# The first four k tiles of a transformer stage scaled and shifted one at a time

## The chip, the cores and the metric

The kernel runs on one core of one Trainium2 chip. The metric is device time in microseconds (us) of one execution. A core has five engines that run side by side, each in the order of its own queue: TensorE (PE: matrix products into PSUM, with PEld its weight loads), VectorE (DVE), ScalarE (ACT), GpSimd (POOL) and SyncE (SP), which here only issues DMA transfers. An engine that needs another's result waits at a semaphore, and everything behind that instruction in its queue waits too.

## The reference, cut to what matters

The reference is a two-layer transformer with a latent stream `lat` and a context stream `cx`, each of 256 tokens and 1024 features; layer 0 has a short convolution as its mixer, layer 1 attention. All of it is float32. The change touches only the first feed-forward block of layer 0, whose input is normalised and modulated:

```
def _rms(t, g):
    t32 = t.astype(jnp.float32)
    y = t32 * lax.rsqrt(jnp.mean(t32 * t32, axis=-1, keepdims=True) + NORM_EPS)
    return y.astype(t.dtype) * g

def _modulate(t, g, shift, scale):
    return _rms(t, g) * (1 + scale) + shift

def _swiglu(h, w13, w2):
    gte, up = jnp.split(h @ w13, 2, axis=-1)
    return (jax.nn.silu(gte) * up) @ w2

mod = (jax.nn.silu(c) @ mod_w[i] + mod_b[i]).reshape(bsz, 3, 3, 1, D_MODEL)
lat = lat + 0.5 * mod[:, 0, 2] * _swiglu(_modulate(lat, norm_g[i, 0], mod[:, 0, 0], mod[:, 0, 1]), ...)
```

Shift and scale are themselves a product: a vector (`silu(c)` for `lat`, `silu(c_ctx)` for `cx`) by 1024 columns of `mod_w` each. So before the first product of the feed-forward block can run, the kernel must have the token norms, and of shift and scale the features that this product reads.

## The kernel before, in words

Features lie on the 128 partitions, so 1024 features are eight k tiles (`KT`), and the 512 tokens of both streams lie side by side in a row (`T2`; `s` = 0 for `lat`, 1 for `cx`). Every float32 matrix is split into a rounded high part and the remainder (`split`, or steps H and D below), and a product is three matmuls: high by high, high by low, low by high.

The first stage multiplies three blocks of 256 hidden columns of `ffn_w13` (i = 0, 1, 2; each a gate half `pg` and an up half `pu`) by all eight k tiles: 3 x 8 x 2 x 3 = 144 matmuls of 128x128 weights by 512 columns. Its order on PE, DVE, ACT and SP is written out by hand, in the string `FIRST_STEPS` (L39), and played under a manual schedule (L1135 to L1139). A step is a letter and digits:

- `L ch q` (`mod_load`, L928) issues on SP the load of two tiles of `mod_w`, 512 KB each: for ch = 1 the scale, for ch = 0 the shift, of the two k tiles 2q and 2q + 1. `R i hf` (`first_raw`) issues the load of half a weight block, 512 KB.
- `P ch q` (`mod_pe`, L934) multiplies them on PE: eight matmuls whose weights are only 32 columns wide (`sccol`), each in one of four column strips of the array (`tile_position=(0, g)`), by 256 columns. The profile shows two records for each of them, as float32 goes through in two passes. The four strips leave partial sums on different partitions.
- `T q` (`mod_turn`, L950) copies these sums out of PSUM (ACT, `row`, L954), turns them into columns and adds up the strips with two small matmuls (PE, L956), and adds the bias (DVE, L963): A00 is 1 + scale, B00 the shift, two k tiles at a time.
- `X` (`first_inv`, L1012) takes the sums of squares and makes the reciprocal norms: a square root (ACT, L1015), a reciprocal (DVE, L1019), two small matmuls for each stream that spread it over all partitions (PE, L287), and a copy out of PSUM for each stream (ACT, `ris`, L1023).
- `U q` (`scale_q`, L1028) multiplies x by gain and reciprocal norm (DVE, `hr`, L1033) for two k tiles and both streams. `N q j` (`norm_one`, L1038) applies A00 and B00 to one k tile: the rounded high part `hh` (ACT, L1043), the exact value (DVE L1049 or ACT L1053), the remainder `hl` (DVE, L1057).
- `H i p` rounds a quarter of weight block i (ACT, `wh`, L1108), `D i p` takes its remainder (DVE, `wl`, L1110), `W` does both.
- `h`, `w`, `l` with i, q, j are two of the stage's matmuls each (L1070), for block i and k tile 2q + j: high by high, low weights by `hh`, high weights by `hl`. `M i q` is all twelve of a pair of k tiles. `F n` is n matmuls on constants that only keep PE busy.

Each engine takes its instructions in the order of the string. SP's loads are gated: `first_sums` (L968) writes one column of the first `mod_w` tile from x (L995), so no load of `mod_w` is issued before that part of x has landed. After the stage, a planner orders DVE and ACT; PE goes on with block i = 3 (L136 to L138).

Of the kernel before, what the change touches and what calls it, by code (L numbers as in the profile page):

```python
# [36 lines left out]


FIRST_STEPS = (  # L39
# [5 lines left out]
)  # L45


# [1 line left out]
def hybrid_kernel(ctx: ExitStack, tc: tile.TileContext, a: dict, out: bass.AP):  # L49
    nc = tc.nc  # L50
# [4 lines left out]
    gp = ctx.enter_context(tc.tile_pool(name="gp", bufs=8))  # L55
    tp = ctx.enter_context(tc.tile_pool(name="tp", bufs=2))
# [32 lines left out]
    eps_t = const.tile([P, 1], F32, name="eps_t", tag="eps_t")  # L89
# [194 lines left out]
    def rms_all(pq, ri):  # L284

        for i in range(2):
            every.append(nc.tensor.matmul(  # L287
                pq[:, i * P : i * P + P], ri[:, i : i + 1].to_broadcast([P, P]), ident,
                start=True, stop=True,
            ).ins)  # L290
        return pq[:, :S]
# [23 lines left out]
    def hot(s, dt=F32R):  # L315
        return hop.tile([P, 1024], dt, name=nm(s), tag="hop")
# [11 lines left out]
    class Beside:  # L328
# [12 lines left out]
    def beside(t):  # L341
        return t[:, :S], t[:, S:], t
# [569 lines left out]
    h32 = {}  # L912
# [7 lines left out]
    A00 = const.tile([P, KT, 2], F32, name="A00", tag="A00")  # L920
    B00 = mod_tile(0, 0)
    sb1 = const.tile([P, KT], F32, name="sb1", tag="sb1")
    def both(t):
        return t.unsqueeze(2).to_broadcast([P, 2, 2])

    rows = {}

    def mod_load(ch, q):  # L928
        if (ch, q) not in rows:
            rows[ch, q] = [hot("pm", F32) for _ in range(2)]  # L930
        for i in range(2):
            nc.sync.dma_start(rows[ch, q][i], a["mod0"][ch, q, :, i * 1024 : i * 1024 + 1024])

    def mod_pe(ch, q):  # L934


        raws = rows[ch, q]
        if ch:
            rows[q] = psum("pr") if q == 0 else psmall("pr")
        pr = rows[q]  # L940
        c = 2 if ch else 0
        for k in range(KT):
            g = 32 * (k % 4)
            o = k % 4 * S
            nc.tensor.matmul(
                pr[g : g + 32, :S], sccol[:, k, c : c + 32], raws[k // 4][:, o : o + S],
                start=(ch == 1 and k < 4), stop=(ch == 0 and k >= 4), tile_position=(0, g),
            )

    def mod_turn(q):  # L950

        pr = rows[q]
        row = tp.tile([P, T2], F32, name=nm("row"), tag="gm", bufs=3)
        nc.scalar.copy(row[:, :S], pr[:, :S])  # L954
        for j in range(2):
            nc.tensor.matmul(  # L956
                pr[:, S + 4 * j : S + 4 * j + 4], row[:, j * P : j * P + P], rowsum,
                start=True, stop=True,
            )
        k2 = slice(2 * q, 2 * q + 2)  # L960
        turned = pr[:, S : S + 8].rearrange("p (k c v) -> p k c v", k=2, c=2)
        for ch in (1, 0):
            nc.vector.tensor_tensor(  # L963
                out=(A00 if ch else B00)[:, k2, :], in0=turned[:, :, 1 - ch, :],
                in1=both(sb1[:, k2] if ch else modb[:, 0, k2]), op=ALU.add,
            )

    def first_sums():  # L968

        pq = psmall("ss")  # L970
        sq = []

        def square(k, eng):
            tag = "gm" if k % 4 < 2 else "sg"
            t = tp.tile([P, T2], F32, name=nm("sq"), tag=tag, bufs=3)
            if eng is nc.vector:
                nc.vector.tensor_tensor(out=t, in0=x[:, k, :], in1=x[:, k, :], op=ALU.mult)
            else:
                nc.scalar.activation(out=t, in_=x[:, k, :], func=AF.Square)
            sq.append(t)  # L980

        def add():
            a, b = sq[-2:]
            nc.vector.tensor_tensor(out=a, in0=a, in1=b, op=ALU.add)
            n = len(sq)
            for i in range(4):
                nc.tensor.matmul(
                    pq[:, i * P : i * P + P], a[:, i * P : i * P + P], ones,
                    start=(n, i) == (2, 0), stop=(n, i) == (KT, 3), skip_group_check=True,
                )  # L990

        square(0, nc.scalar)
        square(1, nc.vector)
        rows[1, 0] = [hot("pm", F32) for _ in range(2)]
        nc.vector.tensor_copy(rows[1, 0][0][:, :1], x[:, 2, :1])  # L995
        add()
        square(2, nc.scalar)
        square(3, nc.scalar)
        add()
        nc.scalar.activation(out=sccol[:, :, 2:4], in_=ccol, func=AF.Silu)  # L1000
        square(4, nc.scalar)
        square(5, nc.vector)
        add()
        square(6, nc.scalar)
        square(7, nc.scalar)
        add()
        nc.vector.tensor_scalar(
            out=sb1, in0=modb[:, 0, KT : 2 * KT], scalar1=1.0, scalar2=None, op0=ALU.add
        )
        return pq  # L1010

    def first_inv(pq):  # L1012

        rs = tp.tile([P, 4], F32, name=nm("rs"), tag="rs4", bufs=1)
        nc.scalar.activation(  # L1015
            out=rs, in_=pq[:, ::P], func=AF.Sqrt, scale=1.0 / D, bias=eps_t
        )
        ri = tp.tile([P, 4], F32, name=nm("ri"), tag="ri4", bufs=1)
        nc.vector.reciprocal(ri, rs)  # L1019
        t = tp.tile([P, T2], F32, name=nm("ris"), tag="ris", bufs=1)  # L1020
        for s in range(2):
            ris.append(t[:, s * S : s * S + S])
            nc.scalar.copy(ris[s], rms_all(psmall("ri") if s else pq, ri[:, 2 * s : 2 * s + 2]))  # L1023

    def raw_of(k, s):
        return h32[k // 2, s][:, (k % 2) * S : (k % 2) * S + S]

    def scale_q(q):  # L1028
        for s in range(2):
            h32[q, s] = gp.tile([P, T2], F32, name=nm("hr"), tag="gl" if s else "gh")  # L1030
        for k in range(2 * q, 2 * q + 2):
            for s in range(2):
                nc.vector.scalar_tensor_tensor(  # L1033
                    out=raw_of(k, s), in0=x[:, k, s * S : s * S + S],
                    scalar=normg[:, 0, 0, k : k + 1], in1=ris[s], op0=ALU.mult, op1=ALU.mult,
                )
# [22 lines left out]
            )  # L1059

    pps = {}
    ris = []

    def first_part(lo):
        def part(i, q, j):
# [16 lines left out]
    ws, gs0, raws, cut = {}, [], {}, {}  # L1082
# [18 lines left out]
    def first_w(part):  # L1101
# [21 lines left out]
        "W": first_w("W"),  # L1123
        "H": first_w("H"),
        "D": first_w("D"),
        "X": lambda: first_inv(pqs),
        "U": scale_q,
        "N": norm_one,
        "h": first_part(0),
# [134 lines left out]
    pqs = pss.tile([P, T2], F32, tag="sm", name="pqs")  # L1264
# [107 lines left out]
    pq = [q_proj(0)]  # L1372
# [17 lines left out]
    for kv in range(KVH):  # L1390
# [7 lines left out]
        out=scq, in0=rq[:, :16], scalar1=float(P) ** -0.5, scalar2=None, op0=ALU.mult  # L1398
# [131 lines left out]
def _layout(inp):  # L1530
    f = lambda k: np.asarray(inp[k])
    d = {}

    def kp(w, width):
# [8 lines left out]
    ccol = d["c2"].reshape(2, KT, P).transpose(2, 1, 0)  # L1543
    mw = f("mod_w")
    m0 = mw[0][:, : 2 * D].reshape(KT, P, 2, 4, S)
    d["mod0"] = m0.transpose(2, 3, 1, 0, 4).reshape(2, 4, P, 2048)
    d["modT"] = mw.transpose(0, 2, 1).reshape(2, 36, 2, P, D).transpose(0, 1, 3, 2, 4).reshape(2, 36, P, 2048)
    modb = f("mod_b").reshape(2, 72, P).transpose(2, 0, 1)
    normg = f("norm_g").reshape(2, 3, KT, P).transpose(3, 0, 1, 2)
# [11 lines left out]
        axis=2,  # L1561
# [48 lines left out]
```

## Time and profile before

| | us |
|---|---|
| median of 3 runs | 1549.24 (1548.73 to 1550.27) |
| the profiled execution | 1548.97 |
| its span in the trace | 1547.2 |
| PE busy | 1533.5 |
| DVE busy | 1298.2 |
| ACT busy | 852.2 |

The span runs from the first to the last instruction; the profiled execution's own time is 1.8 us longer. Rows of the timeline have the start (us), the time taken (us), the engine, the line of the kernel, the operation, output<-inputs, the shape, how many instructions the row holds, and in brackets how long the engine had been idle and what ended that. A "q" behind an engine is its sequencer, which issues DMAs. The time of a matmul reaches from its start to the end of its way through the array; the next one may start before. Lines are those of the kernel before.

### The profile page before, as it was taken

The page shows a single profiled execution, that of the slowest core. Times are in us where ns is not written, and L with a number is a line of the kernel's source. Part 1 is how long each engine was busy: PE and PEld are TensorE (multiplying, and loading weights), DVE is VectorE, ACT ScalarE, POOL GpSimd, SP SyncE. Part 2 cuts the span into 40 slices and gives each one's busy share as a digit, 9 for nine tenths or more (in the row PEclk, how much of TensorE's full clock was granted, in tenths as well). Part 3 has the DMA queues.
Part 4 walks back from the last instruction along what each step waited for, and adds up shares of the span by engine and source line. Part 5 has one row for each costly group of instructions (what it writes and reads, how often), then busy time and mean ns, then how long its engine had stood idle before and what let it go on. Part 6 is the DMA issues. An engine that isn't in the chain of part 4 may idle for free.

```text
span 1547.2 us, 27333 instructions
## 1 busy us (share of the span) xinstructions
PE 1533.5 (99%) x10594; PEld 1423.6 (92%) x10594; DVE 1298.2 (84%) x1964; ACT 852.2 (55%) x1468; POOL 301.3 (19%) x265
## 2 busy tenths in 40 slices
PE   8999999999999999999999999999999999999999
PEld 6898998999999899989999899989999899998888
DVE  5888788898989999968979889958968788998676
ACT  5644554645655376446456466446456456774553
POOL 0013313402231023042052112043042002300000
PEclk9999999999999999999999999999999999999999
DMA  9568768765356636695796625785697743476562
GB/s 377 199 188 235 162 184 232 164 194 143 75 143 175 206 91 151 212 216 135 213 214 153 207 68 136 220 189 138 210 220 182 253 159 114 142 246 220 170 195 76
DMA packets 97474, 278.80 MB, mean 180 GB/s; under 512 B 11456, under 2 KB 13120, under 8 KB 97344
## 3 DMA queue, kind: packets, MB, share of 16 engines
q1 hardware_dynamic: 69408, 228.10, 45.4%
q0 software_dynamic: 25920, 47.20, 18.1%
q10 hardware_dynamic: 2016, 1.76, 0.4%
q8 instruction: 83, 1.36, 0.4%
q14 instruction: 47, 0.39, 0.1%
HBM read 262.07 MB, written 1.05 MB: 170 GB/s over the span
## 4 chain that ended last, share of the span: by engine, by line
PE 89%; DVE 6%; DMA 2%; ACT 1%; issue 1%; POOL 0%; SPq 0%; DVEq 0%; POOLq 0%; ACTq 0%
PE p L138 8%; PE p L137 8%; PE p L136 8%; PE py L137 8%; PE py L136 8%; PE py L138 8%; PE q L138 6%; PE q L136 6%; PE q L137 6%; PE py L144 2%; PE pu L144 2%; PE pg L144 2%; DVE wl L108 1%; DMA wr<-in_w 1%; PE py L146 1%
## 5 line engine op out<-in xcount | busy, mean ns | idle before, releaser
L107 ACT ACTIVATE wh<-wr 128x1024 fp32r<-128x1024 f32 (+2 forms) x454 | 400.5, 909 | 289.2 <-PE py L137 94.5
L108 DVE TENSOR_TENSOR wl<-wr,wh 128x1024 fp32r<-128x1024 f32 (+2 forms) x454 | 468.6, 1056 | 107.0 <-ACT wh L107 87.0
L177 DVE CUSTOM_DVE_ANT_0 junk<-wr,scbc,first 128x1024 bf16<-128x1024 f32 x209 | 269.9, 1291 | 2.2 <-DMA wr<-in_modT 0.2
L137 PE MATMUL py<-gl,wh 128*128 128x512 f32 (+1 forms) x570 | 213.4, 374 | 0.0
L136 PE MATMUL py<-gh,wh 128*128 128x512 f32 (+1 forms) x570 | 213.4, 374 | 0.0
L138 PE MATMUL py<-gh,wl 128*128 128x512 f32 (+1 forms) x570 | 212.8, 373 | 0.0
L709 POOL TENSOR_SCALAR wr<-wr 128x512 f32<-128x512 f32 x66 | 125.4, 1900 | 424.0 <-DMA wr<-in_w 162.7
L136 PE MATMUL p<-th,wh 128*128 128x256 f32 x528 | 149.5, 283 | 0.0
L138 PE MATMUL p<-th,wl 128*128 128x256 f32 x528 | 149.4, 283 | 0.0
L137 PE MATMUL p<-tl,wh 128*128 128x256 f32 x528 | 149.4, 283 | 0.0
L138 PEld LDWEIGHTS py<-gh,wl 128*128 128x128 f32 x570 | 107.3, 188 | 19.1
L136 PEld LDWEIGHTS py<-gh,wh 128*128 128x128 f32 x570 | 107.4, 188 | 18.3
L137 PEld LDWEIGHTS py<-gl,wh 128*128 128x128 f32 x570 | 107.4, 188 | 18.2
L138 PE MATMUL q<-bh,wl 128*128 128x256 f32 x400 | 113.2, 283 | 0.0
L137 PE MATMUL q<-bl,wh 128*128 128x256 f32 x400 | 113.2, 283 | 0.0
L136 PE MATMUL q<-bh,wh 128*128 128x256 f32 x400 | 113.2, 283 | 0.0
L136 PEld LDWEIGHTS p<-th,wh 128*128 128x128 f32 x528 | 101.3, 192 | 0.4
L137 PEld LDWEIGHTS p<-tl,wh 128*128 128x128 f32 x528 | 101.3, 192 | 0.4
L138 PEld LDWEIGHTS p<-th,wl 128*128 128x128 f32 x528 | 101.3, 192 | 0.0
L114 POOL DMA_DIRECT2D w4l<-in_w x56 | 53.2, 949 | 229.9 <-ACT w4l L113 183.5
L566 POOL DMA_DIRECT2D x<-yg x48 | 44.7, 995 | 215.7 <-ACT yg L563 172.4
L772 ACT ACTIVATE sg<-sg 128x512 f32<-128x512 f32 x56 | 35.3, 631 | 89.0 <-DVE sg L768 88.9
(321 smaller groups left out, 4199.4 us busy)
## 6 DMA issues: line engine op xcount, KB each, us to landing
wr<-in_w SPq DMA_DIRECT2D x120, 512.0 KB, 4.8
wr<-in_modT SPq DMA_DIRECT2D x113, 512.0 KB, 5.1
wr<-in_w2b SPq DMA_DIRECT2D x64, 448.0 KB, 4.0
wr<-in_w2a SPq DMA_DIRECT2D x32, 512.0 KB, 4.4
wr<-in_w SPq DMA_DIRECT2D x56, 256.0 KB, 4.6
wr<-in_w POOLq DMA_DIRECT2D x56, 256.0 KB, 6.0
w4l<-in_w POOLq DMA_DIRECT2D x56, 256.0 KB, 5.8
x<-yg POOLq DMA_DIRECT2D x48, 256.0 KB, 7.6
```

The source lines that it names most:

```text
L107: nc.scalar.activation(out=hi, in_=src, func=AF.Copy)
L108: return nc.vector.tensor_tensor(out=lo, in0=src, in1=hi.bitcast(F32), op=ALU.subtract)
L114: nc.gpsimd.dma_start(out=lo, in_=src, accum_op=ALU.add)
L136: nc.tensor.matmul(ps, wh, mh, start=first, stop=False, **kw)
L137: nc.tensor.matmul(ps, wh, ml, start=False, stop=False, **kw)
L138: return nc.tensor.matmul(ps, wl, mh, start=False, stop=last, **kw).ins
L144: nc.tensor.matmul(ps, w[0], m[2], start=first and n == 0, stop=False)
L146: nc.tensor.matmul(ps[:, :S], w[1], m[0], start=False, stop=last and n == len(ms) - 1)
L177: nc.vector.tensor_tensor_reduce(out=junk, in0=raw, in1=scbc[:, v, :], scale=0.5 if ch in (2, 8) else 1.0, scalar=modb[:, l, col : col + 1 ...
L566: nc.gpsimd.dma_start(out=x[:, m, :], in_=t, accum_op=ALU.add)
L709: nc.gpsimd.tensor_scalar(out=r1[:, :T2], in0=r2[:, :T2], scalar1=-1.0, scalar2=None, op0=ALU.mult)
L772: nc.scalar.activation(out=self.sg, in_=self.sg, func=AF.Silu)
```

## The change

The steps that concern the first four k tiles (q = 0 and 1) can now be given a third digit, j, and are then done for one k tile alone:

- The host lays out `mod_w` for q = 0 and 1 by k tile, so that one 512 KB tile holds all 1024 rows of 128 columns (one k tile's scale, or its shift). `L ch q j` loads one such tile. The bytes are the same.
- `P ch q j` is eight matmuls by 128 columns in place of eight by 256.
- `T q j` copies 128 columns, makes one small matmul and two adds.
- `U q j` scales one k tile.
- `X` is split in two: `X0` makes square root, reciprocal and the spreading matmuls of stream 0, `X1` those of stream 1. Their results stay in PSUM, and the first scaling (`U00`) reads them there. A new step `Y` (`first_keep`) copies both to SBUF later, behind N00 and the rounding of two quarters each of blocks 0 and 1.
- The gate of the first `mod_w` load reads x's k tile 1 in place of 2, that is the first of four loads of x in place of the second; and it stands ahead of DVE's first square.
- The string is rewritten. Ahead of the first product stand `P100 X0 P000 X1 U00 T00 F4 H00 N00 H01`; k tile 1 has its own `P101 P001 T01` amid the products of k tile 0, k tiles 2 and 3 have `P110 P010 T10` and `P111 P011 T11`; `P12` and `P02` stand apart, with six products between, and `T2` directly behind `P02`; `P13 P03` and `T3` are as they were. Loads are issued in the new order too: `L100 L000 R00 R10 L101 L001 R20 L110 L010 L111 L12 L011 R01 R11 L13 L02 L03 R21`.

Behind the stage, PE, POOL and SP keep their order. On ACT and DVE the first instructions behind the stage are ordered otherwise: the silu of block 0 (L664) and its product (L666) now stand ahead of the split of block 3's weights (L107, L108).

```diff
 FIRST_STEPS = (
-    "L10 L00 R00 R10 X U0 P10 L11 P00 L01 F2 T0 W00 N00 W01 N01 F5 h000 w000 l000 R20 W10 "
-    "W11 h001 w001 h100 h101 l001 l100 l101 U1 H20 H21 P11 L12 P01 L02 w100 w101 h200 T1 D20 D21 "
-    "N10 N11 h201 l200 l201 w200 w201 U2 h010 w010 l010 R01 R11 P12 L13 P02 L03 h011 w011 l011 T2 "
-    "M11 R21 N20 N21 W02 W03 W12 W13 U3 h210 w210 l210 P13 P03 h211 w211 l211 T3 W22 W23 M02 "
-    "N30 N31 M12 M22 M03 M13 M23 S"
+    "L100 L000 R00 R10 L101 L001 P100 X0 P000 X1 U00 T00 F4 H00 N00 H01 D00 h000 D01 H10 H11 l000 h100 "
+    "w000 R20 Y U01 P101 L110 P001 L010 l100 T01 H20 D10 D11 D20 w100 U10 N01 H21 h001 w001 D21 h101 w101 L111 "
+    "P110 L12 P010 L011 l001 T10 l101 N10 h200 h201 U11 l200 l201 w200 w201 h010 w010 P111 P011 l010 h110 "
+    "w110 T11 l110 N11 U2 R01 R11 P12 L13 L02 h011 w011 l011 P02 L03 T2 h111 w111 l111 R21 N20 N21 W02 W03 W12 "
+    "W13 U3 h210 w210 l210 P13 P03 h211 w211 l211 T3 W22 W23 M02 N30 N31 M12 M22 M03 M13 M23 S"
 )
...
-    def mod_pe(ch, q):
+    def mod_pe(ch, q, j=None):
...
+        n = S if j is None else P
+        to = 0 if j is None else j * P
         for k in range(KT):
             g = 32 * (k % 4)
-            o = k % 4 * S
+            raw, o = (raws[k // 4], k % 4 * S) if j is None else (raws[j], k * P)
             nc.tensor.matmul(
-                pr[g : g + 32, :S], sccol[:, k, c : c + 32], raws[k // 4][:, o : o + S],
+                pr[g : g + 32, to : to + n], sccol[:, k, c : c + 32], raw[:, o : o + n],
...
-    def mod_turn(q):
+    def mod_turn(q, *js):
...
-        nc.scalar.copy(row[:, :S], pr[:, :S])
-        for j in range(2):
+        nc.scalar.copy(row[:, a * P : b * P], pr[:, a * P : b * P])
+        for j in js:
...
         square(0, nc.scalar)
+        rows[1, 0] = [hot("pm", F32) for _ in range(2)]
+        nc.vector.tensor_copy(rows[1, 0][0][:, :1], x[:, 1, :1])
         square(1, nc.vector)
-        rows[1, 0] = [hot("pm", F32) for _ in range(2)]
-        nc.vector.tensor_copy(rows[1, 0][0][:, :1], x[:, 2, :1])
...
+    def first_inv(s):
+
+        if s == 0:
+            rs = tp.tile([P, 4], F32, name=nm("rs"), tag="rs4", bufs=1)
+            nc.scalar.activation(
+                out=rs, in_=pqs[:, ::P], func=AF.Sqrt, scale=1.0 / D, bias=eps_t
+            )
+            ri4.append(tp.tile([P, 4], F32, name=nm("ri"), tag="ri4", bufs=1))
+            nc.vector.reciprocal(ri4[0], rs)
+        ris.append(rms_all(psmall("ri") if s else pqs, ri4[0][:, 2 * s : 2 * s + 2]))
+
+    def first_keep():
+
         t = tp.tile([P, T2], F32, name=nm("ris"), tag="ris", bufs=1)
         for s in range(2):
-            ris.append(t[:, s * S : s * S + S])
-            nc.scalar.copy(ris[s], rms_all(psmall("ri") if s else pq, ri[:, 2 * s : 2 * s + 2]))
+            nc.scalar.copy(t[:, s * S : s * S + S], ris[s])
+            ris[s] = t[:, s * S : s * S + S]
...
-    def scale_q(q):
+    def scale_q(q, *js):
...
     m0 = mw[0][:, : 2 * D].reshape(KT, P, 2, 4, S)
-    d["mod0"] = m0.transpose(2, 3, 1, 0, 4).reshape(2, 4, P, 2048)
+    m0 = m0.transpose(2, 3, 1, 0, 4)
+    by_k = m0[:, :2].reshape(2, 2, P, KT, 2, P).transpose(0, 1, 2, 4, 3, 5)
+    d["mod0"] = np.concatenate([t.reshape(2, 2, P, 2048) for t in (by_k, m0[:, 2:])], axis=1)
```

More of the change, by code (lines that the diff above doesn't have):

```diff
@@ L922, in hybrid_kernel, with both, mod_load @@
     sb1 = const.tile([P, KT], F32, name="sb1", tag="sb1")
-    def both(t):
-        return t.unsqueeze(2).to_broadcast([P, 2, 2])
+    def both(t, n):
+        return t.unsqueeze(2).to_broadcast([P, n, 2])
     rows = {}
-    def mod_load(ch, q):
+    def mod_load(ch, q, *js):
         if (ch, q) not in rows:
             rows[ch, q] = [hot("pm", F32) for _ in range(2)]
-        for i in range(2):
+        for i in js or range(2):
             nc.sync.dma_start(rows[ch, q][i], a["mod0"][ch, q, :, i * 1024 : i * 1024 + 1024])
-    def mod_pe(ch, q):
+    def mod_pe(ch, q, j=None):
         raws = rows[ch, q]
-        if ch:
+        if ch and not j:
             rows[q] = psum("pr") if q == 0 else psmall("pr")
@@ L941, in mod_pe @@
         c = 2 if ch else 0
+        n = S if j is None else P
+        to = 0 if j is None else j * P
         for k in range(KT):
             g = 32 * (k % 4)
-            o = k % 4 * S
+            raw, o = (raws[k // 4], k % 4 * S) if j is None else (raws[j], k * P)
             nc.tensor.matmul(
-                pr[g : g + 32, :S], sccol[:, k, c : c + 32], raws[k // 4][:, o : o + S],
+                pr[g : g + 32, to : to + n], sccol[:, k, c : c + 32], raw[:, o : o + n],
                 start=(ch == 1 and k < 4), stop=(ch == 0 and k >= 4), tile_position=(0, g),
             )
-    def mod_turn(q):
+    def mod_turn(q, *js):
         pr = rows[q]
+        js = js or (0, 1)
+        a, b = js[0], js[-1] + 1
         row = tp.tile([P, T2], F32, name=nm("row"), tag="gm", bufs=3)
-        nc.scalar.copy(row[:, :S], pr[:, :S])
-        for j in range(2):
+        nc.scalar.copy(row[:, a * P : b * P], pr[:, a * P : b * P])
+        for j in js:
             nc.tensor.matmul(
@@ L959, in mod_turn @@
             )
-        k2 = slice(2 * q, 2 * q + 2)
-        turned = pr[:, S : S + 8].rearrange("p (k c v) -> p k c v", k=2, c=2)
+        k2 = slice(2 * q + a, 2 * q + b)
+        turned = pr[:, S + 4 * a : S + 4 * b].rearrange("p (k c v) -> p k c v", k=b - a, c=2)
         for ch in (1, 0):
@@ L964, in mod_turn @@
                 out=(A00 if ch else B00)[:, k2, :], in0=turned[:, :, 1 - ch, :],
-                in1=both(sb1[:, k2] if ch else modb[:, 0, k2]), op=ALU.add,
+                in1=both(sb1[:, k2] if ch else modb[:, 0, k2], b - a), op=ALU.add,
             )
@@ L1010, in first_sums @@
         return pq
[L1012 to L1019, printed above, removed]
+    def first_inv(s):
[8 more added lines that the diff above has]
+    def first_keep():
         t = tp.tile([P, T2], F32, name=nm("ris"), tag="ris", bufs=1)
         for s in range(2):
-            ris.append(t[:, s * S : s * S + S])
-            nc.scalar.copy(ris[s], rms_all(psmall("ri") if s else pq, ri[:, 2 * s : 2 * s + 2]))
+            nc.scalar.copy(t[:, s * S : s * S + S], ris[s])
+            ris[s] = t[:, s * S : s * S + S]
     def raw_of(k, s):
         return h32[k // 2, s][:, (k % 2) * S : (k % 2) * S + S]
-    def scale_q(q):
+    def scale_q(q, *js):
         for s in range(2):
-            h32[q, s] = gp.tile([P, T2], F32, name=nm("hr"), tag="gl" if s else "gh")
-        for k in range(2 * q, 2 * q + 2):
+            if (q, s) not in h32:
+                h32[q, s] = gp.tile([P, T2], F32, name=nm("hr"), tag="gl" if s else "gh")
+        for k in [2 * q + j for j in js or range(2)]:
             for s in range(2):
@@ L1061, in hybrid_kernel @@
     pps = {}
-    ris = []
+    ris, ri4 = [], []
     def first_part(lo):
@@ L1125, in hybrid_kernel @@
         "D": first_w("D"),
-        "X": lambda: first_inv(pqs),
+        "X": first_inv,
+        "Y": first_keep,
         "U": scale_q,
```

## The prediction

> **What bounds the kernel now.** I read the page's first part and its chain of waits, then busy time by stretches, cut where the first stage's first and last products stand, and then the timeline of the first 30 us.
>
> ```profile
> PE 1533.5 (99%) x10594; PEld 1423.6 (92%) x10594; DVE 1298.2 (84%) x1964; ACT 852.2 (55%) x1468; POOL 301.3 (19%) x265
> ...
> PE 89%; DVE 6%; DMA 2%; ACT 1%; issue 1%; POOL 0%; SPq 0%; DVEq 0%; POOLq 0%; ACTq 0%
> ```
> ```profile
> core 0: us, PE busy (x) PEld busy (x) DVE busy (x) ACT busy (x) POOL busy (x), PEclk, DMA share, GB/s
> 0.00:18.67 18.67, 14.68 (x114) 12.21 (x114) 7.86 (x21) 9.60 (x18) 0.19 (x4) 1.00 0.89 333
> 18.67:60.44 41.77, 41.28 (x252) 30.86 (x253) 31.68 (x69) 29.73 (x52) 0.00 (x0) 1.00 0.87 341
> 60.44:229.50 169.06, 169.06 (x1097) 155.28 (x1096) 143.28 (x194) 83.70 (x142) 38.79 (x35) 1.00 0.69 184
> ```
>
> PE is busy for 99% of the span and the chain lies on it for 89%. The second row is the changed stage, from its first product to the first one behind it: 41.77 us, of which PE is idle for 0.5. Behind it PE has no idle time at all up to 229.5. So whatever the change adds to or takes from PE's queue up to 60.44 moves the rest with it: I add up when the last product of this stage goes.
>
> The head, up to the first product, is a chain of short steps:
>
> ```profile
> 11.54 0.28 PE L987 MATMUL ss<-ones,sq 128*128 128x128 f32 x1
> ...
> 12.38 0.71 PE L287 MATMUL ss<-first,ri 128*128 128x128 f32 x4 [0.57 <-DVE ri L1019]
> 12.93 0.61 PE L287 MATMUL ri<-first,ri 128*128 128x128 f32 x4
> ...
> 13.54 1.73 DVE L1033 SCALAR_TENSOR_TENSOR hr<-x,first,ris 128x256 f32<-128x256 f32 x4 [1.21 <-ACT ris L1023]
> ...
> 15.43 0.64 PE L945 MATMUL pr<-pm,sccol 128*32 128x256 f32 x8 [0.45 <-DMA pm<-in_mod]
> ...
> 16.13 0.37 ACT L954 COPY row<-pr 128x256 f32<-128x256 f32 x1 [2.18 <-PE pr L945]
> ...
> 16.56 0.61 PE L956 MATMUL pr<-first,row 128*128 128x4 f32 x4
> ...
> 17.26 0.16 DVE L963 TENSOR_TENSOR A<-pr,sb 128x4 f32<-128x4 f32 x1 [1.99 <-ACT row L954]
> ...
> 17.41 0.68 DVE L1110 TENSOR_TENSOR wl<-wr,wh 128x512 fp32r<-128x512 f32 x1
> ...
> 17.53 1.09 ACT L1043 ACTIVATE hh<-hr,mod,A 128x256 fp32r<-128x256 f32 x2 [0.25 <-DVE mod L963]
> ...
> 18.16 0.91 DVE L1049 TENSOR_SCALAR hr<-hr,A,mod 128x256 f32<-128x256 f32 x2
> ...
> 18.53 0.62 ACT L1108 ACTIVATE wh<-wr 128x512 fp32r<-128x512 f32 x1
> ...
> 18.67 0.50 PE L1070 MATMUL pg<-hh,wh 128*128 128x512 f32 x1 [0.29 <-ACT hh L1043]
> ...
> 18.98 0.75 DVE L1057 TENSOR_TENSOR hl<-hr,hh 128x256 fp32r<-128x256 f32 x2
> ...
> 20.39 0.50 PE L1070 MATMUL pu<-hh,wl 128*128 128x512 f32 x1 [0.47 <-DVE wl L1110]
> ...
> 20.73 0.40 PE L1070 MATMUL pg<-hl,wh 128*128 128x512 f32 x1
> ```
>
> The last of four `mod_w` tiles lets PE start again at 15.43; copy, turn, adds and rounding follow, and the first product starts at 18.67. The fifth starts at 20.73: four products at 0.23 are 0.91, so 1.15 of these 2.06 us are waits. From there PE runs without a wait worth counting. What a step P and a step T cost amid the products, and where the stage ends, is seen here:
>
> ```profile
> L945 PE MATMUL pr<-pm,sccol x128: 379/379/404, 13.5 to 41.8; 128*32 128x256 f32 x128
> ```
> ```profile
> 24.19 0.39 PE L1070 MATMUL pu<-hl,wh 128*128 128x512 f32 x1
> ...
> 24.51 1.93 PE L945 MATMUL pr<-pm,sccol 128*32 128x256 f32 x32
> ...
> 26.37 0.50 PE L1070 MATMUL pg<-hh,wl 128*128 128x512 f32 x1
> ...
> 26.71 0.40 PE L1070 MATMUL pu<-hh,wl 128*128 128x512 f32 x1
> ...
> 27.63 0.39 PE L1070 MATMUL pu<-hh,wh 128*128 128x512 f32 x1
> ...
> 27.86 0.50 PE L956 MATMUL pr<-first,row 128*128 128x4 f32 x4
> ...
> 28.55 0.40 PE L1070 MATMUL pu<-hh,wh 128*128 128x512 f32 x1
> ...
> 60.44 0.39 PE L136 MATMUL pg<-hh,wh 128*128 128x512 f32 x1
> ```
>
> From 24.19 to 26.71 are 2.52 us for two product times (0.46) and 32 P records: a pair of P steps adds 2.06. The 32 records hold eight groups of four (one per column strip); a record itself lasts 0.38 (the row ahead), so the starts spread over 1.55 and a group takes 0.216. Eight of them are 1.73; the other 0.33 is the price of a break, entering and leaving the narrow form. From 27.63 to 28.55 are 0.92 for two products and a T: T adds 0.46.
>
> **The change, part by part.** *Head.* P100 runs between the sums and the reciprocal, where PE idles 0.57, and costs nothing unless its load is late. The loads that count are these:
>
> ```profile
> L932 SPq DMA_DIRECT2D pm<-in_mod x2: 432/432/433, 6.7 to 7.2; - x2
> ...
> DMA to landing us min/median/max: 6.2/6.6/7.0
> ```
>
> The second tile of `mod_w` lands at 6.7 + 6.2 = 12.9, the third transfer at 7.2 + 7.0 = 14.2. In the new order these are L000 and R00. X0 takes PE from 12.4 to 12.85, P000 starts at about 13.0 in either case, and its four groups end at 13.6. So the earlier gate brings nothing I can name; the later loads are ahead of their use by 2 us and more. A group of 128 columns should take half of 0.216, and the spreading matmuls of 128 columns do go every 0.112 ((0.61 - 0.28)/3: the first row there is one matmul of that form, 0.28 long). I take 0.112; the upper bound is the 0.216 of whole ones, nothing being saved. X1 13.6 to 14.2; U00 for stream 1 then 14.3 to 14.8 on DVE (0.43 from SBUF by the 1.73 for four; from PSUM I add 0.05, bounds 0 and 0.2). T00 is done by 14.5, but its adds stand behind U00 on DVE: 14.8 to 15.0. Two roundings (1.09) end at 16.13: first product at 16.18, 2.49 earlier. H01 stands behind these roundings on ACT (0.62), so the second product waits 0.32; the remainder hl (0.91 + 0.75 from 15.7, DVE) comes at 17.27, another 0.36; 0.06 for D01. Eight products and 0.74 of waits take the place of four and 1.15: 0.41 more. Lead: 2.90.
>
> *P steps amid the products.* Before: three pairs at 2.06, 6.18. After: P101 P001, P110 P010 and P111 P011 at 8 x 0.112 + 0.33 = 1.23 each; P12 and P02, each alone, 4 x 0.216 + 0.33 = 1.19; P13 P03 2.06. Together 8.13: +1.95. Half of k tile 1's work came from the head, and two breaks more are paid.
>
> *T steps.* Three at 0.46 before; after three of one small matmul (two records fewer at 0.112: 0.24) and two at 0.46: +0.26.
>
> *New waits.* T01 needs the copy behind P001 (P001 done 19.9, copy of 128 columns 0.27 between the bounds 0.2 and 0.37) and starts at 20.4. Its adds come at 20.9, and behind them on DVE stand D10 and D11, whose weights were rounded long before: at 0.68 and then 0.61 each they are done at 21.85 and 22.45. PE, free at 20.7, has w100 next: waits of 1.20 and 0.27. Behind w100 stand h001 and all else. l011 needs the remainder of k tile 3, which comes 2.7 us after T11's adds: two roundings and two affine passes on ACT at 0.54, then hl at 0.45. PE has 2.3 us of work until then (l110, P12, four products): 0.44. T2 directly behind P02 waits for the last group, the copy (0.37) and two handovers: 0.53. Together 2.44, against 0.14 of small waits in that stretch before.
>
> *Hidden.* Y's two copies (0.37 each) run on ACT from 17.6 to 18.4 while PE is on l000 to w000; U01 behind them ends at 19.3, before T01. At the stage's end block 0's silu and product precede the split of block 3's weights:
>
> ```profile
> L107 ACT ACTIVATE wh<-wr 128x1024 fp32r<-128x1024 f32 x4 | 4.1, 1045 | 0.0
> ...
> L108 DVE TENSOR_TENSOR wl<-wr,wh 128x1024 fp32r<-128x1024 f32 x3 | 3.6, 1225 | 0.0
> ```
>
> Block 0's last product stands 24 products (5.5 us) ahead of block 3's first; silu some 0.65, then 1.05 and 1.23 are 2.9. Its cover is 2.6 us; without it PE would stall by the excess alone.
>
> *Sum.* -2.90 + 1.95 + 0.26 + 2.44 - 0.14 = +1.6. The profiled execution, 1548.97, becomes 1550.6; the median of the runs is 0.27 above it, so I predict 1550.9, slower by 0.1%. 0.2% is about 3.1 us, about what a measurement of this kernel can tell from no change.
>
> The Trainium skill has a rule that speaks against halving: by "TensorE: Matmul & The Clock Gate", section "Wait — 56ns, not 53.3ns?", a sequencer without hardware decode spends about 62 ns on each matmul, which binds once the array's work is shorter. An estimate by that page: 16 records would then take 0.99 in place of 0.45, six such halves amid the products +3.2, and the kernel would stand at some 1554.5. The trace disagrees as far as it goes: the eight records at 15.43, issued straight after a wait, spread over 0.26, 37 ns each. No run here shows groups of 128.
>
> **The rivals.** *Halving saves nothing* (24%). If a group of 128 columns still takes 0.216, weight loads or issue being the bound, 24 groups amid the products cost 0.104 more each (2.5), and P100 and P000 delay the first product by 0.8: +4.9, 1554.2. For it: the 32-column weights of each record are reloaded whatever the columns. Against it: the 0.112 above, with larger weights. It passes 0.2% once a group takes more than about 0.16.
>
> *The early gate delays x* (6%). The first `mod_w` load now goes while x still comes; if it shares the way, the last x tile lands later, and sums, root and all behind follow one to one. One tile is 1.24 (14.2 less 12.9): up to +2.8, 1552.1. Against it: the four transfers of x, issued within 1.4 us, landed one after another, from 0.7 + 4.2 = 4.9 to 2.1 + 6.6 = 8.7.
>
> ```profile
> L86 SPq DMA_DIRECT2D x<-in_xT x4: 387/422/610, 0.7 to 2.1; - x4
> ...
> DMA to landing us min/median/max: 4.2/5.4/6.6
> ```
>
> *The delay is absorbed* (9%). Later in the kernel PE waits for ACT and DVE:
>
> ```profile
> PE pg L136 <- ACT bh L391: 1.4, 1, 1.4
> PE q L136 <- ACT gm L762: 1.2, 1, 1.2
> ...
> PE q L138 <- DVE wl L108: 1.0, 1, 1.0
> ```
>
> Where these engines do not move with PE, a later PE only waits less: 1.2 at the first and 0.4 at the next use up the 1.6, 1549.2. Against it: DVE's work there is released by PE itself, 40 us earlier or less.
>
> *The new waits are covered* (9%). If adds, copies and remainders go fast enough that PE finds w100, l011 and T2 released, -2.44: 1548.5, on the fast side; with luck downstream it may pass 3.1.
>
> **How the numbers follow.** My forecast has 52%; its own range is 1549.7 to 1552.3 (copy, PSUM and handovers at their bounds, and the spread of runs, 0.8), and I give 7 of the 52 to waits that I missed taking it past 0.2%. Slower: 24 + 7 + half of 6 = 0.34; faster: half of the last rival, 0.05; the same: 0.61. The range runs from 1547.6, below the covered waits' 1548.5 by the spread, to 1555.0, above the first rival's 1554.2.
>
> **What would show it.** Right: first product near 16.2; 16 records of a halved P in some 0.45 plus one record's length; a wait of about 1.2 before w100 for DVE L1120 of the changed kernel; T2 waiting for the copy; the stage's end near 62.0. Wrong: halved groups 0.2 apart; last x tile after 8.7; no waits at w100; PE idle between 60 and 66, for block 3's weights.

## The result, and the profile after

| us | before | after |
|---|---|---|
| median of 17 runs each, on the same chips | 1550.05 (1548.34 to 1551.62) | 1553.2 (1550.67 to 1554.81) |
| span of the profiled execution | 1547.2 | 1551.2 |
| first product of the first stage | 18.67 | 16.69 |
| first product behind it (stage end) | 60.44 | 62.60 |

The changed kernel takes 1.0019 times as long (95% interval 1.0012 to 1.0027): 2.9 us more. A second series of 11 runs gave 1.0015 (1.0007 to 1.0024). The median of before in these runs is 0.8 above the 1549.24 from which the prediction started.

The page of the changed kernel, its part on engines, and its busy time by stretches (start:end and length, then busy time and instructions of PE, PEld, DVE, ACT, POOL; granted clock, DMA share, GB/s), cut at the same two products:

```profile
PE 1535.7 (99%) x10652; PEld 1424.8 (92%) x10652; DVE 1294.3 (83%) x1968; ACT 852.8 (55%) x1470; POOL 301.3 (19%) x265
```
```profile
0.00:16.69 16.69, 13.44 (x106) 11.78 (x106) 6.46 (x18) 8.63 (x16) 0.19 (x4) 1.00 0.90 335
16.69:62.60 45.91, 44.08 (x319) 32.31 (x319) 31.24 (x73) 28.79 (x54) 0.00 (x0) 1.00 0.82 309
62.60:231.66 169.06, 169.06 (x1097) 155.31 (x1096) 144.34 (x197) 85.81 (x145) 37.86 (x35) 1.00 0.73 188
```

The head is 1.98 us shorter. The stage is 4.14 longer (45.91 against 41.77): PE is busy for 2.80 of it and idle for 1.34 more (1.83 against 0.49). The stretch behind is the same to the hundredth. The timeline of the changed kernel shows where:

```profile
9.28 1.15 ACT L983 ACTIVATE sq<-x 128x512 f32<-128x512 f32 x2 [0.59 <-DMA x<-in_xT]
...
12.30 0.65 PE L947 MATMUL pr<-pm,sccol 128*32 128x128 f32 x16
12.93 0.71 PE L287 MATMUL ss<-first,ri 128*128 128x128 f32 x4
...
13.68 0.48 DVE L1043 SCALAR_TENSOR_TENSOR hr<-x,first,ss 128x256 f32<-128x256 f32 x1 [0.80 <-PE ss L287]
...
16.69 0.49 PE L1080 MATMUL pg<-hh,wh 128*128 128x512 f32 x1 [0.71 <-ACT hh L1053]
17.21 0.50 PE L1080 MATMUL pu<-hh,wh 128*128 128x512 f32 x1
...
19.05 0.47 PE L1080 MATMUL pu<-hh,wl 128*128 128x512 f32 x1
19.45 1.08 PE L947 MATMUL pr<-pm,sccol 128*32 128x128 f32 x32
20.46 0.50 PE L1080 MATMUL pg<-hl,wh 128*128 128x512 f32 x1
20.80 0.39 PE L1080 MATMUL pu<-hl,wh 128*128 128x512 f32 x1
21.03 0.28 PE L960 MATMUL pr<-first,row 128*128 128x4 f32 x2
22.23 0.50 PE L1080 MATMUL pg<-hh,wl 128*128 128x512 f32 x1 [0.92 <-DVE wl L1120]
22.83 0.50 PE L1080 MATMUL pu<-hh,wl 128*128 128x512 f32 x1
23.17 0.39 PE L1080 MATMUL pg<-hh,wh 128*128 128x512 f32 x1
...
24.78 0.39 PE L1080 MATMUL pu<-hh,wl 128*128 128x512 f32 x1
25.10 1.08 PE L947 MATMUL pr<-pm,sccol 128*32 128x128 f32 x32
26.11 0.50 PE L1080 MATMUL pg<-hl,wh 128*128 128x512 f32 x1
26.44 0.40 PE L1080 MATMUL pu<-hl,wh 128*128 128x512 f32 x1
...
36.77 0.50 PE L1080 MATMUL pg<-hl,wh 128*128 128x512 f32 x1 [0.20 <-DVE hl L1067]
...
38.99 0.61 PE L960 MATMUL pr<-first,row 128*128 128x4 f32 x4 [0.49 <-ACT row L958]
...
62.60 0.39 PE L136 MATMUL pg<-hh,wh 128*128 128x512 f32 x1
```

The three waits that were forecast are there: w100 at 22.23, l011 at 36.77, T2 at 38.99. From 19.05 to 20.80 are 1.75 us for two product times (0.46) and a pair of halved P steps, so the first pair adds 1.29; the second, from 24.78 to 26.44, adds 1.20, and the third, from 30.78 to 32.44, the same. The last tile of x landed at 9.26 (the last two squares, first row, start on it); in the profile of before that row stands at 8.73.

Behind the stage, the same two products of before and after, in the timeline of each kernel; first before:

```profile
268.63 0.28 PE L138 MATMUL q<-th,wl 128*128 128x256 f32 x1
...
1379.00 0.39 PE L138 MATMUL pg<-zh,wl 128*128 128x258 f32 x1
```
```profile
271.54 0.39 PE L138 MATMUL q<-th,wl 128*128 128x256 f32 x1 [0.59 <-DVE wl L108]
...
1383.06 0.39 PE L138 MATMUL pg<-zh,wl 128*128 128x258 f32 x1 [0.38 <-DVE wl L108]
```

The delay is 2.16 at the stage's end, 2.91 at the first and 4.06 at the second: between these two executions another 1.9 us was lost behind the stage. At the first row PE waits for the low part of a weight tile. DVE could only make that after a load had landed: in the changed kernel it waited 2.07 us for the landing, until 266.11, in the kernel before 1.52 us, until 262.82. In the same place another kernel, the second order without a single k tile (below), waited longer still, though its stage ends earlier than that of the kernel before. Here is its row, and then one product further on, first before, then after, then that order:

```profile
270.29 0.39 PE L138 MATMUL q<-th,wl 128*128 128x256 f32 x1 [2.31 <-DVE wl L108]
```
```profile
391.44 0.39 PE L137 MATMUL pg<-bl,wh 128*128 128x256 f32 x1 [0.41 <-DVE bl L108]
```
```profile
394.89 0.39 PE L137 MATMUL pg<-bl,wh 128*128 128x256 f32 x1 [0.40 <-DVE bl L108]
```
```profile
393.55 0.39 PE L137 MATMUL pg<-bl,wh 128*128 128x256 f32 x1 [0.40 <-DVE bl L108]
```

From the stage's end to this product are 331.00 us before, 332.29 after and 334.04 in that order; over the twelve profiled executions of this document the stretch varied from 331.00 to 334.04, and the profile of before is the shortest. So this part of the loss, 1.29 of the 1.9, needs nothing of the change; the rest comes in later, most of it by the second product above. What a delay alone costs is asked below.

### The profile page after: what moved, and what is told of

The parts are those of the page before. It is cut to its first block, busy times and chain, and to the rows that moved or that the text cites. A ratio compares the mean times of both kernels' runs of the same rounds, so it can differ in the third digit from the quotient of the medians.

```text
span 1551.2 us, 27450 instructions
## 1 busy us (share of the span) xinstructions
PE 1535.7 (99%) x10652; PEld 1424.8 (92%) x10652; DVE 1294.3 (83%) x1968; ACT 852.8 (55%) x1470; POOL 301.3 (19%) x265
## 4 chain that ended last, share of the span: by engine, by line
PE 74%; DVE 5%; ACT 1%; DMA 1%; issue 1%; POOL 0%; DVEq 0%; ACTq 0%; POOLq 0%; SPq 0%
PE p L136 7%; PE p L138 7%; PE p L137 7%; PE py L137 7%; PE py L136 7%; PE py L138 6%; PE q L138 5%; PE q L136 5%; PE q L137 5%; PE py L144 2%; PE pu L144 2%; PE pg L144 2%; DVE wl L108 1%; PE py L146 1%; PE pg L146 1%; PE pu L146 1%
## 5 line engine op out<-in xcount | busy, mean ns | idle before, releaser
L107 ACT ACTIVATE wh<-wr 128x1024 fp32r<-128x1024 f32 (+2 forms) x454 | 400.6, 909 | 283.1 <-PE py L137 93.3
L108 DVE TENSOR_TENSOR wl<-wr,wh 128x1024 fp32r<-128x1024 f32 (+2 forms) x454 | 466.3, 1051 | 107.7 <-ACT wh L107 88.4
```

Source lines behind the costliest of these rows:

```text
L107: nc.scalar.activation(out=hi, in_=src, func=AF.Copy)
L108: return nc.vector.tensor_tensor(out=lo, in0=src, in1=hi.bitcast(F32), op=ALU.subtract)
```

## The experiments

Each kernel ran 11 times beside 21 or 33 runs of before on the same chip. "Stage length" is the time from the first product to the stage's end, which does not hang on when the head came through. For the new orders the whole string is given; in the others only what differs.

### The gate as it was before

```diff
-        rows[1, 0] = [hot("pm", F32) for _ in range(2)]
-        nc.vector.tensor_copy(rows[1, 0][0][:, :1], x[:, 1, :1])
         square(1, nc.vector)
+        rows[1, 0] = [hot("pm", F32) for _ in range(2)]
+        nc.vector.tensor_copy(rows[1, 0][0][:, :1], x[:, 2, :1])
```

> The changed kernel, with the gate of the mod_w loads as it was before (x's k tile 2, behind DVE's first square). Theory (the early gate makes the last two x tiles land 0.55 late, and the head follows): the last tile of x lands at 8.7 in place of 9.26, the square root and all behind it move up, first product at 16.15 in place of 16.69, stage end at 62.05 in place of 62.60, and the time falls by about 0.5 us. Rival (the late x tiles are chance, or the second mod_w tile, which would land at about 12.9, holds the head instead): first product stays at 16.6 to 16.7, end at 62.6, no change in time.

Ratio to before 1.0014 (1.0006 to 1.0023). Its timeline, the last squares and the first product:

```profile
9.41 1.15 ACT L983 ACTIVATE sq<-x 128x512 f32<-128x512 f32 x2 [0.60 <-DMA x<-in_xT]
...
16.83 0.50 PE L1080 MATMUL pg<-hh,wh 128*128 128x512 f32 x1 [0.71 <-ACT hh L1053]
```

The theory fell: with the old gate the last tile of x lands no earlier. But the rival is only half right, since the head does go with that tile. From the last squares to the first product are 7.41 in the changed kernel and 7.42 here.

### The changed kernel once more

> The changed kernel once more, unchanged. If its head goes with the landing of the last x tile and with nothing else, the first product stands 7.43 to 7.44 us behind that landing again, whenever that is (9.15 to 9.45 in the four profiles so far), and the stage's end follows it one to one (62.5 to 62.8). If the head hangs on a load of mod_w or of weights, that distance differs from 7.44 by 0.1 or more. Time: 2 to 4 us above the kernel before.

```profile
9.27 1.15 ACT L983 ACTIVATE sq<-x 128x512 f32<-128x512 f32 x2 [0.61 <-DMA x<-in_xT]
...
16.68 0.50 PE L1080 MATMUL pg<-hh,wh 128*128 128x512 f32 x1 [0.71 <-ACT hh L1053]
```

7.41 again, stage end 62.55, and the time 2.3 us above before. Over twelve profiled executions the last tile of x landed at 8.71, 9.10, 9.14, 9.39 and 9.58 with the old gate and between 8.97 and 9.45 with the new one: 8.71, the profile from which the prediction took its durations, was the earliest of all.

### A pure delay in the kernel before

```diff
-... P11 L12 P01 L02 w100 w101 h200 T1 ...
+... P11 L12 P01 L02 F10 w100 w101 h200 T1 ...
```

> The kernel before, with ten matmuls on constants (step F10) put into PE's queue ahead of w100: nothing else changes, PE is only 2.2 us later (0.22 each). It asks what a later stage end costs behind the stage, where the changed kernel lost another 1 to 1.9 us. Theory 1 (the delay is passed on as it is): stage end at 62.6 to 62.7, time +2.2 us. Theory 2 (the transfers behind the stage do badly with any shift, and add to it): time +2.8 to +4. Theory 3 (waits further down absorb it): time +0.5 to +1.0.

```profile
9.13 1.15 ACT L978 ACTIVATE sq<-x 128x512 f32<-128x512 f32 x2 [0.61 <-DMA x<-in_xT]
...
15.47 0.16 PEld L944 LDWEIGHTS pr<-pm,sccol 128*32 128x32 f32 x8 [0.59 <-DMA pm<-in_mod]
...
18.72 0.49 PE L1069 MATMUL pg<-hh,wh 128*128 128x512 f32 x1 [0.28 <-ACT hh L1042]
...
26.43 2.50 PE L917 MATMUL idle<-ones 128*128 128x128 f32 x20
...
62.74 0.39 PE L135 MATMUL pg<-hh,wh 128*128 128x512 f32 x1
```

(Lines are one lower in this kernel.) The stage ends 2.30 late and the ratio is 1.0020 (1.0011 to 1.0029): 3.1 us, 1.7 to 4.5. That is what the changed kernel shows for 2.16. So nothing in the change but its delay is needed for the loss behind the stage; whether a delay is passed on as it is, or with half a microsecond more, these runs can't tell (theories 1 and 2 both lie in the interval, theory 3 does not). The first three rows say something else: with x 0.4 later than in the first profile, before's first product is only 0.05 later. Its head waits for the last of the four loads of `mod_w` (the second row; PE idled 0.45 for it in the first profile), and x hides behind that.

### D10 and D11 ahead of T01's adds

```diff
-w000 R20 Y U01 P101 ... T01 H20 D10 D11 D20 w100 ...
+w000 R20 Y U01 D10 D11 P101 ... T01 H20 D20 w100 ...
```

> The changed kernel with D10 and D11 moved ahead of P101 in the string, so that on DVE they stand ahead of T01's two adds. Theory (w100 waits 0.92 + 0.37 for DVE only because of these two remainders behind the adds): w100 starts right behind T01 at about 21.3, the rest follows, stage end 61.3 to 61.4, time -1.2 us. Rival (the wait belongs to the chain T01, adds, rounding of k tile 1, and only changes its name): h001 waits about 1.0 for hh in place of w100, stage end 62.1 to 62.3, time -0.3 to -0.5 us.

```profile
20.92 0.28 PE L960 MATMUL pr<-first,row 128*128 128x4 f32 x2
21.06 0.48 PE L1080 MATMUL pg<-hh,wl 128*128 128x512 f32 x1
21.37 0.40 PE L1080 MATMUL pu<-hh,wl 128*128 128x512 f32 x1
22.64 0.51 PE L1080 MATMUL pg<-hh,wh 128*128 128x512 f32 x1 [0.87 <-ACT hh L1053]
```

The rival held. w100 no longer waits, and h001 behind it waits 0.87 for the rounding of k tile 1. Stage length 45.62 (62.21 less 16.59) against 45.91: of the 1.45 us that the waits at w100 cost, 0.29 are gained. PE has too little work between T01 and the first product that needs it; which instruction shows the wait is a matter of order. Ratio 1.0014 (1.0005 to 1.0023).

### T2 behind six products

```diff
-... P02 L03 T2 h111 w111 l111 R21 ...
+... P02 L03 h111 w111 l111 T2 R21 ...
```

> The changed kernel with T2 moved behind the six products h111 w111 l111 that followed it. Theory (its wait of 0.5 for the copy is then hidden): stage end at 62.05, time -0.5 us. Rival (the adds behind T2 then come 1 us later on DVE, with them the rounding of k tiles 4 and 5 on ACT and the copy of T3, which stands behind these): T3 waits about 1.1 for its copy, stage end 62.6 to 63.3, time 0 to +0.7 us.

```profile
38.64 0.50 PE L1080 MATMUL pg<-hh,wh 128*128 128x512 f32 x1
...
46.45 0.61 PE L960 MATMUL pr<-first,row 128*128 128x4 f32 x4 [0.85 <-ACT row L958]
```

The rival held: T2's wait is gone and T3 waits 0.85 in its place. ACT takes the adds' rounding, then four roundings of weights, then the copy for T3: all of it moved back with T2. The stage is 46.45 long, 0.54 more than the changed kernel's, and the ratio the highest of all, 1.0025 (1.0016 to 1.0034).

### k tiles 2 and 3 as a pair

```diff
-... P101 L110 P001 L010 l100 ... U10 ... L111 P110 L12 P010 L011 l001 T10 l101 N10 ... U11 ... P111 P011 ... T11 ...
+... P101 L11 P001 l100 ... U1 ... L01 P11 L12 P01 l001 T1 l101 N10 ...
...
-    by_k = m0[:, :2].reshape(2, 2, P, KT, 2, P).transpose(0, 1, 2, 4, 3, 5)
-    d["mod0"] = np.concatenate([t.reshape(2, 2, P, 2048) for t in (by_k, m0[:, 2:])], axis=1)
+    by_k = m0[:, :1].reshape(2, 1, P, KT, 2, P).transpose(0, 1, 2, 4, 3, 5)
+    d["mod0"] = np.concatenate([t.reshape(2, -1, P, 2048) for t in (by_k, m0[:, 1:])], axis=1)
```

> The changed kernel with k tiles 2 and 3 (q = 1) laid out, loaded, multiplied, turned and scaled as a pair, as before; k tiles 0 and 1 stay single. Theory (what is done singly amid the products is paid in breaks): one pair of P steps at 2.06 takes the place of two at 1.20, and the wait at l011 goes: 0.34 + 0.36, stage end at 61.8 to 62.0 for an x tile at 9.3, time -0.7 us against the changed kernel. Rival (the whole pair comes too late for the products of k tile 2 and opens a new wait): a wait over 0.5 at l101, l001 or h010 and an end at 62.6 or later.

First product 16.89, end 62.06, so the stage is 45.17 long: 0.74 less, against 0.70 by the row sums (0.34 + 0.36). No new wait came. Ratio 1.0009 (1.0001 to 1.0018).

### New orders, with the single k tile and without

First with k tiles 0 and 1 single and q = 1 whole (layout as in the last experiment):

```
L100 L000 R00 R10 L101 L001 P100 P000 R20 X0 T00 H00 X1 F4 U00 H01 N00 D00 H10 h000 P101 l000 Y L11 H11 P001 D01 U01
h100 T01 D10 H20 l100 H21 w000 h200 D11 N01 l200 w100 U1 L01 w001 w101 h201 l101 P11 L12 P01 D21 l001 l201 R01 R11
D20 T1 P12 h101 w201 N11 w111 w211 U2 h211 h001 w011 N10 w110 U3 w200 h111 W12 l011 L13 l211 h010 L02 l110 P02 W03
h011 T2 L03 R21 W02 P13 P03 h210 T3 l111 N20 W13 l010 w010 N30 l210 h110 N21 W22 M12 W23 N31 w210 M22 M02 M13 M23 M03 S
```

> k tiles 0 and 1 single, q = 1 whole, and the order of the steps chosen anew so that by the durations of the rows no product waits: adds of T00 ahead of U00, both quarters of block 0 rounded before h000, products of block 2 between T01 and h001, T2 and T3 behind six products each. Theory (the single k tile gives the lead, and the rest of the loss is waits and breaks): first product 7.0 us behind the last x tile (16.2 to 16.4), no wait over 0.2 after it, stage end at 58.7 to 59.3, 1.1 to 1.7 ahead of the kernel before, and the time 1 to 2 us below it. Rival (the waits come back at other places, as for T2 and D10): stage end at 60 or later, no gain.

First product 16.52, stage end 60.51, ratio 1.0002 (0.9993 to 1.0011). By the terms set down, the rival held: the stage ends no earlier than that of the kernel before, 1.2 to 1.8 us behind the forecast, though the stage itself is 1.18 shorter than in the last experiment. Two waits came back, 0.41 for a remainder hl at 45.24 and 0.46 at the stage's end, where block 3's first product waits for the silu of block 0, whose last products stood at the very end (M03).

The kernel before, by the same means:

```
L10 X L00 R00 R10 P10 L11 U0 P00 F2 T0 W01 F5 W00 N00 W10 h000 w000 W11 L01 h100 l100 N01 l000 R20 h001 w001 U1 w100
P11 L12 P01 l001 h101 L02 w101 l101 T1 H20 H21 h200 l200 R01 R11 l201 N10 N11 h201 P12 L13 P02 D20 L03 D21 R21 h210
U2 M11 l011 l010 w211 w201 T2 P13 P03 W13 l211 N20 T3 W03 W02 N21 h010 w210 W12 h211 l210 U3 W23 N31 w200 w011 W22
M02 M12 h011 w010 N30 M13 M22 M23 M03 S
```

> The kernel before, no k tile single, only the order of the steps of the first stage chosen anew by the same durations. If order alone makes the gain: first product at 18.7 as before, then no wait over 0.2, stage end at 59.2 to 59.5, time about -1 us. If the kernel before had no slack in its order: stage end at 60.4, no change.

Neither: the stage ends at 61.97, later than before. Three waits, 0.47 for a load of `mod_w` at 38.55, 0.79 for hl at 51.22, and 0.46 for block 0's silu again. Ratio 1.0014 (1.0005 to 1.0023).

Both again, with the last products of block 0 (M03) ahead of others, and more products between each N and what reads it. With the single k tile:

```
L100 L000 R00 R10 L101 L001 P100 P000 X0 T00 H00 H01 X1 F4 R20 U00 N00 H11 h000 H10 Y P101 U01 D10 l000 L11 P001 D11
h100 T01 l100 H21 H20 w100 D20 D21 L01 N01 h200 l200 w101 h001 h201 U1 h101 l001 D00 P11 L12 P01 R01 R11 l201 w201
D01 U2 T1 N10 P12 l101 N11 W03 w000 h010 L13 w200 h210 U3 h110 l110 W02 w001 w010 w011 L02 h011 l011 w211 W12 w210
h111 W13 P02 L03 h211 l211 R21 T2 P13 P03 N20 l210 T3 N21 l010 w111 W22 l111 w110 M02 W23 M12 N31 N30 M22 M03 M23 M13 S
```

> A second order for k tiles 0 and 1 single and q = 1 whole; against the first one, block 0's last products stand 24 ahead of block 3's first (there, the first product of block 3 waited 0.46 for the silu of block 0), and ten products stand between N20 and the first product that reads it. If these two waits were what kept the first one at 60.5: stage end at 59.2 to 59.9, and a time 0.3 to 1.3 us below the kernel before, which three rounds more or less can't tell from no change. If waits turn up at other places again: end at 60.3 or later.

Without it:

```
L10 L00 R00 R10 P10 X L11 P00 U0 F2 T0 F5 W01 W00 N00 h000 W10 L01 W11 R20 w000 h100 l100 N01 l000 h101 h001 w100 U1
P11 L12 P01 w001 l101 T1 H21 w101 L02 H20 N10 R01 h200 l201 R11 h201 D20 l200 h210 U2 D21 N11 P12 W13 L13 P02 L03
h011 h010 h211 W03 W12 W02 R21 l010 w211 M11 T2 N20 P13 P03 w210 w010 T3 l210 N21 l211 U3 w201 w011 W23 W22 N31 M12
M02 l001 N30 l011 M03 M22 w200 M13 M23 S
```

> The same for the kernel before (no single k tile, order alone, block 0's last products early): first product at 18.7 to 19.0. If the single k tile is what gains: stage end 0.5 us or more behind that of the other order, at 60.0 to 60.6. If order alone does it: 59.4 to 59.8, and the lead of two us at the first product buys nothing because PE has less work between the waits later.

Busy time by stretches, cut at first product and stage end, first with the single k tile, then without:

```profile
0.00:15.98 15.98, 13.29 (x106) 11.91 (x106) 6.30 (x18) 9.14 (x17) 0.19 (x4) 1.00 0.88 327
15.98:59.32 43.34, 42.89 (x287) 31.72 (x287) 32.86 (x73) 28.94 (x53) 0.00 (x0) 1.00 0.91 349
```
```profile
0.00:19.15 19.15, 15.52 (x114) 12.57 (x115) 8.18 (x21) 10.01 (x19) 0.19 (x4) 1.00 0.90 332
19.15:59.51 40.36, 40.36 (x253) 31.20 (x254) 30.41 (x69) 29.60 (x52) 0.00 (x0) 1.00 0.86 339
```

Both end their stage ahead of the kernel before, by 1.12 and 0.93. The single k tile starts 3.17 earlier and ends 0.19 earlier: its stage is 2.98 longer. Of that, 2.1 are work by the prediction's row sums: P101 and P001 stand apart (0.45 + 0.33 each) and P12 and P02 too (1.19 each), 8.06 with the two pairs left at 2.06, against three pairs, and T01 adds 0.24. Another 0.7 is a wait of h200 for its weights (19.98 to 21.17 are 1.19 us for two products of 0.23; the 0.45 in brackets counts only from the end of the last product's way through the array):

```profile
19.98 0.40 PE L1080 MATMUL pu<-hh,wl 128*128 128x512 f32 x1
20.83 0.50 PE L1080 MATMUL pg<-hh,wh 128*128 128x512 f32 x1 [0.45 <-ACT wh L1118]
21.17 0.39 PE L1080 MATMUL pu<-hh,wh 128*128 128x512 f32 x1
```

In time they stand at 0.9998 (0.9989 to 1.0007) and 0.9995 (0.9986 to 1.0004) of before: ahead in the trace, not told from no change by the runs. Of the two readings set down for the order without the single k tile, the second held (an end at 59.4 to 59.8): order alone brings what there is, and the earlier first product buys nothing that these runs can show.

| kernel | first product | stage end | stage length | time, ratio to before |
|---|---|---|---|---|
| before | 18.67 | 60.44 | 41.77 | 1 |
| after | 16.69 | 62.60 | 45.91 | 1.0019, 1.0015 |
| after, old gate | 16.83 | 62.71 | 45.88 | 1.0014 |
| before, delayed | 18.72 | 62.74 | 44.02 | 1.0020 |
| D10, D11 first | 16.59 | 62.21 | 45.62 | 1.0014 |
| T2 apart | 16.88 | 63.33 | 46.45 | 1.0025 |
| q = 1 whole | 16.89 | 62.06 | 45.17 | 1.0009 |
| first new order, single | 16.52 | 60.51 | 43.99 | 1.0002 |
| first new order, not single | 19.05 | 61.97 | 42.92 | 1.0014 |
| second, single | 15.98 | 59.32 | 43.34 | 0.9998 |
| second, not single | 19.15 | 59.51 | 40.36 | 0.9995 |

## Why the prediction was right in most, and where it was not

**The frame held.** The time follows when the last product of the stage goes: over the eleven kernels the ratios rise with the stage's end, within their intervals, from 0.9998 and 0.9995 at 59.3 and 59.5 to 1.0025 at 63.3. The sign was right, the time lies in the range, and the ratio lies at the 0.2% that I had set as the bound: "the same" was the larger chance, and 1.0019 with its interval can't say on which side it is. The range was wide, though: it reached to 1555.0 for the sake of a rival that fell. My forecast's own range, 1549.7 to 1552.3, was missed by 0.9.

**The terms of the sum.** By the rows shown above:

| term | forecast | measured |
|---|---|---|
| first product | 16.18 | 16.69 |
| waits among the first eight products | 0.74 | 0.76 |
| a halved pair amid the products | 1.23 | 1.29, and twice 1.20 |
| w100, both | 1.47 | 1.45 (20.80 to 23.17, less three products and T01 at 0.23) |
| l011 | 0.44 | 0.36 |
| T2's wait | 0.53 | 0.49 |
| stage length | 45.9 (62.04 less 16.18) | 45.91 |
| stage end, against before | +1.6 | +2.16 |

One small term came out right by luck: a scaling out of PSUM, forecast at 0.48 as 0.43 from SBUF and 0.05 for PSUM. The 0.43 was a mean over four scalings that overlap (1.73 for four). One by one they last the same, from PSUM (`ss`) as from SBUF (`ris`), in the changed kernel (ns of one, least, median, most):

```profile
L1043 DVE SCALAR_TENSOR_TENSOR hr<-x,first,ris x14: 476/480/482, 18.9 to 47.2; 128x256 f32<-128x256 f32 x14
L1043 DVE SCALAR_TENSOR_TENSOR hr<-x,first,ss x1: 481/481/481, 13.7 to 13.7; 128x256 f32<-128x256 f32 x1
```

**The step that failed** is in the head: "X0 takes PE from 12.4 to 12.85", and with it "first product at 16.18". The chain behind was right within 0.04: 7.47 from the last tile of x (8.71) to the first product was forecast, 7.43 was measured (9.26 to 16.69). But the landing of x was taken from one execution, in which it was the earliest of twelve. In the kernel before that tile hides behind a load of `mod_w`; the change takes that load off the path and puts the head on x, one to one. I had priced a late x under the rival "the early gate delays x". The delay came; the gate does not make it, as the kernel with the old gate shows. Of the 0.56 by which the stage's end missed the forecast, 0.51 are this.

**The rest of the miss** lies outside the stage. Of the 2.3 us between 1550.9 and 1553.2, 0.8 is before's own median, 1550.05 in place of 1549.24. Behind the stage the profiled executions differ by 1.9, the medians by some 0.8 (2.9 less 2.16), and a pure delay of 2.30 gave 3.1. I had forecast that a delay would be passed on one to one, with 9% for its being absorbed; it is not absorbed. Whether it grows is open: single executions differ more behind the stage (331.00 to 334.04) than the amount in question.

**The rivals.** *Halving saves nothing* fell: the next product follows 1.01 us behind the first of 32 records of two halved steps (19.45 to 20.46), and the starts of P100's 16 records spread over 0.37 (0.65 less 0.27 for the last one). In the trace the four records of a group start 7 ns apart, and a group follows the last one by 0.110 us. So the 62 ns for each matmul without hardware decode, which the Trainium skill gives in "TensorE: Matmul & The Clock Gate", section "Wait — 56ns, not 53.3ns?", are not the bound here; whether this chip decoded in hardware, no run shows. *The new waits are covered* fell as well: all three stood where they were forecast. What I had wrong is the cause of the largest: the wait at w100 was put down to DVE's queue (D10 and D11), and without these it moved to h001 and only 0.29 of it went.

**What the change does, then.** It moves the turn of k tile 1 out of the head, where PE had nothing else to do, into the stage, where PE is the bound. The lead of two to three us is real, and is more than paid back, in breaks between narrow and wide matmuls, in more P and T steps, and in the waits that each turn brings. With k tiles 2 and 3 kept in pairs and the order chosen anew, the single k tile's stage ends 0.19 us ahead of the best order without it. That is one execution of each, and less than the landing of x varies by (0.87), and in time the two can't be told apart: no gain from the single k tile is shown.

## What to carry to other kernels

An earlier start is worth only what it does not add to the engine that bounds the rest: price the work that is moved out of an idle stretch at its full cost in the busy one. A wait of a static order belongs to a chain and not to the instruction that shows it, so before moving an instruction, ask which one waits next. And when a change takes one of two arrivals off the path, look up how much the other one varies from execution to execution; one profile does not tell.

## What the runs showed that I had not expected

The landing of the last tile of x, a 512 KB load issued at 2.1 us, varied from 8.71 to 9.58 between executions that issue the same four loads of x at the same times; the gate does not order them, and what does is open. Groups of four narrow matmuls went every 0.11 us at 128 columns, and the weight load of 32 columns, 105 to 111 ns, is as long as that. My guess is that halving the columns again would save nothing; no kernel here tried it.

The weight loads and matmuls of the P steps in the changed kernel, by line (ns of one, least, median, most):

```profile
L947 PEld LDWEIGHTS pr<-pm,sccol x192: 105/110/111, 12.3 to 43.8; 128*32 128x32 f32 x192
L947 PE MATMUL pr<-pm,sccol x192: 272/273/405, 12.3 to 44.0; 128*32 128x128 f32 x128, 128*32 128x256 f32 x64
```
